# SP's transfers in program order, bias lines on GpSimd, late stores, and a first pair projected side by side

## The chip, the core and the metric

The kernel runs on one core of one Trainium2 chip. TensorE (PE) multiplies matrices into PSUM, VectorE (DVE) and ScalarE (ACT) work on vectors, GpSimd (POOL) does masks and simple sums, and SyncE (SP) issues the transfers between HBM and SBUF. Every engine has its own queue and takes its instructions in order; they meet at semaphores. The metric is the time of one execution in microseconds, as the device measures it; lower is better.

## The reference

One step of a two-layer encoder over 256 prompt frames and 32 sample frames, 288 columns in all, each of 1024 features, in float32:

```
layer 0: x += [chunked attention (8 heads, relative bias) | stick-breaking attention (8 heads)](rmsnorm(x)) @ w_out_ab
layer 1: x += forgetting attention (16 heads, softmax(q k / 8 + cumulative log-forget bias))(rmsnorm(x)) @ w_out_c
each   : x += cross-attention to 256 memory rows (4 heads);   x += (silu(h w_gate) * (h w_up)) w_down
y = rmsnorm(x)
```

The sample frames attend to caches as well. Beside `y` the kernel must return the keys and values of every attention (`kv0`, `kv1`), the log forget values (`lf`) and the memory keys and values (`mkT`, `mv`). The bias of the chunked heads is a table of 257 values a head, indexed by the clipped distance between query and key.

## The kernel before

**Tiles and units.** Activations lie with features on partitions: `x` is 8 tiles of 128 x 288. A weight unit is 128 x 1024 floats (512 KB): the 8 blocks that give 128 output features. Each product is made in three matmuls from a high and a low half (`mm3`, line 145): `unit` (line 132) loads a unit into one of 4 `st` buffers, ScalarE casts it to `hi` (5 buffers), VectorE subtracts to get `lo` (4 buffers). A unit is 24 matmuls; `project` (line 151) does them into one of 4 PSUM banks called `pj`. The normalised input is not scaled by its row's root mean square before the projection: `Next.block` gives x times gain as `hh` and `hl`, and the scale `rstd` (called `cur.r`) is applied when a bank is evicted (`evac_q`, `evac_kv`, `gate`). What is evicted before `rstd` is known waits in a list (`cur.then`).

**Order of work.** The program is one traced sequence. After every unit `project` calls `tick` (line 176), which advances every active generator by one step: norms (`scale`, line 272: `columns`, that is the matmuls `nrm`, then a step later `rows`, that is `nr`), attention heads (`attend_prompt`, line 359: transpose v, scores, softmax; next step transposes `tp`; next step the product `po`), the gate of layer 1 (line 821), memory preparation. A planner then fixes each engine's own order by an estimate of when each instruction is ready and in which order it was traced; it may let an instruction that is ready pass one that is not, on SP too. So in the kernel before, loads may pass stores that wait for their data.

**Start.** `first_part` loads the first unit in three parts between the x tiles (lines 79 to 86). The first three units (q, k and v of pair 0) are projected one after another. 32 small matmuls ahead (line 120) run while the first data arrives. `rel_lines` (line 735) makes the bias table of the chunked heads in DRAM: a line of 384 values a head, written 128 times at a row step of 385, so that rows of 384 read back show it shifted by one each; `rel_prompt` loads two pieces for a head.

**Layers.** `mix_ab` and `mix_c` run `pairs` (line 807): for each of 8 pairs of heads three units, then the pair's attention becomes active, every second pair the sample's too; `memory.steps` puts units of the memory projection between them. `mix_c` first does the gate's unit; the gate's step behind the unit of k0 ends in the two `lf` stores (lines 848, 849), and two steps later it stores cumulative sums in DRAM (`cumd`, `cumsd`), which `attend` of `mix_c` reads back. Then `out_project`, `cross` and `ffn`. In `cross`, `sample` loads four cache tiles into 4 `ca` buffers.

**Names in the profile.** `pj` projections, `op` and `dn` output projections, `mv` memory values, `vt`, `sc`, `tp`, `po` a pair's attention, `gt`, `gc`, `gs`, `gn` the gate, `st` weight loads, `skew` and `bi` the bias.

Of the kernel before, what the change touches and what calls it, by code (L numbers as in the profile page):

```python
# [15 lines left out]
P = 128  # L16
# [6 lines left out]
FB = 22  # L23


@with_exitstack
def encoder_step(ctx: ExitStack, tc: tile.TileContext, a):
# [15 lines left out]
    cnt = [0]  # L43

# [29 lines left out]
    first = wp.tile([P, 1024], F32, tag="st", bufs=4, name="first")  # L74

    def first_part(c0, c1):
        DMA.dma_start(first[:, c0:c1], a["w_ab"][0][:, c0:c1])

    first_part(0, 256)
# [12 lines left out]
    make_identity(nc, identb)  # L92

# [23 lines left out]
    for h in range(4):  # L117
        G.memset(odd[32 * h:32 * h + 32, h % 2:h % 2 + 1], 1.0)

# [12 lines left out]
    def unit(src, st=None, pieces=1):  # L132

        if st is None:
            st = wp.tile([P, 1024], F32, tag="st", bufs=4, name=name("st"))
            DMA.dma_start(st, src)
        hi = wp.tile([P, 1024], F32R, tag="hi", bufs=5, name=name("hi"))
        lo = wp.tile([P, 1024], F32R, tag="lo", bufs=4, name=name("lo"))
        for c in range(pieces):
            b = slice(c * 1024 // pieces, (c + 1) * 1024 // pieces)  # L140
            S.copy(hi[:, b], st[:, b])  # L141
            V.tensor_tensor(lo[:, b], st[:, b], hi[:, b].bitcast(F32), ALU.subtract)  # L142
        return hi, lo
# [7 lines left out]
    def project(src, h, n=NT, w=None, begun=None):  # L151
        if begun:
            w, p = begun
        else:
            w, p = w or unit(src), acc("pj")
        with tc.issue_after(warmed.ins):
            for k in range(BEGIN if begun else 0, KT):
                mm3(p[:, :n], w, k, h, k, k == 0, k == KT - 1)
        tick()
        return p  # L160
# [24 lines left out]
    def finish():  # L185
        while active:
            tick()
# [65 lines left out]
    class Next:  # L253
# [86 lines left out]
    def softmax(s, cols, bias, out):  # L340
# [3 lines left out]
        for i, (c0, c1) in enumerate(cols):  # L344
# [4 lines left out]
            else:  # L349
                V.tensor_tensor_reduce(out=out[:, c0:c1], in0=s[:, c0:c1], in1=bias[:, c0:c1], scale=-1.0, scalar=3e38,  # L350
# [8 lines left out]
    def attend_prompt(q, k, v, vns, j, bias, oh, ol):  # L359

        vn = vns[j] = v_natural(v)
        e = []
        for hd in range(2):
# [5 lines left out]
            softmax(s, QT, bias[hd], e[hd])  # L369
# [134 lines left out]
    def cache(src):  # L504
        t = wk.tile([P, 512], F32, tag="ca", bufs=4, name=name("ca"))
        DMA.dma_start(t, src)
        return t
# [11 lines left out]
    class Memory:  # L519
# [5 lines left out]
        def prepare(self):  # L525

            for c in range(2):
                st = wp.tile([P, 1024], F32, tag="st", bufs=4, name=name("mem"))
                DMA.dma_start(st, a["memT"][:, 1024 * c:1024 * c + 1024])
# [14 lines left out]
        def step(self):  # L544
            i, l = self.i, self.l
            self.i += 1
            if i < 8:
# [5 lines left out]
                DMA.dma_start(a["mkT"][l, i], t[:, 0:NP])  # L553
                self.k.append(split(t[:, 0:NP], tok("kh", F32R)[:, 0:NP], tok("kl", F32R)[:, 0:NP]))
            else:
# [13 lines left out]
                if half == 1:  # L569
                    for t in range(2):  # L570
                        v = tok("mv")
                        V.tensor_scalar(v[:, 0:NP], self.p[:, 256 * t:256 * t + 256], memcol[:, t:t + 1], None, op0=ALU.mult)
                        DMA.dma_start(a["mv"][l, t, :, hd * 256:hd * 256 + 256], v[:, 0:NP])
# [151 lines left out]
    def evac_kv(cur, p, dst):  # L725
        t = tok("kv")

        def go():
            V.tensor_tensor(t, p[:, :NT], cur.r, ALU.mult)
            DMA.dma_start(dst, t)  # L730
# [4 lines left out]
    def rel_lines():  # L735


        ln = cst.tile([8, 384], F32, name="line")
        DMA.dma_start(ln[:, 128:384], a["rel"][:, 0:256])
        V.tensor_copy(ln[:, 0:128], ln[:, 128:129].to_broadcast([8, 128]))  # L740
        d = dr.tile([8, 384], F32, name="lined")
        DMA.dma_start(d, ln)
        sk = dr.tile([8, 128 * 385], F32, name="skew")
        for h in range(8):
            DMA.dma_start(bass.AP(tensor=sk.tensor, offset=sk.offset + h * 128 * 385, ap=[[385, P], [1, 384]]),
                          bass.AP(tensor=d.tensor, offset=d.offset + 384 * h, ap=[[0, P], [1, 384]]))
        return sk

    def rel_rows(sk, h, c, rows, n):

        return bass.AP(tensor=sk.tensor, offset=sk.offset + h * 128 * 385 + c, ap=[[384, rows], [1, n]])

    def rel_prompt(sk, h):
        t = wk.tile([P, 384], F32, tag="bi", bufs=5, name=name("bi"))
        DMA.dma_start(t[:, 0:128], rel_rows(sk, h, 256, P, 128))
        DMA.dma_start(t[:, 128:384], rel_rows(sk, h, 128, P, 256))
        G.memset(t[0:64, 64:128], NEG)
        G.memset(t[0:64, 320:384], NEG)
        return t

    def rel_sample(sk, g):
        t = wk.tile([P, 384], F32, tag="bi", bufs=5, name=name("bs"))
        for h in range(4):
            DMA.dma_start(t[32 * h:32 * h + 32, 0:160], rel_rows(sk, 4 * g + h, 128, NS, 160))
        return t

    def mix_ab(cur, nxt, memory, w0):
# [3 lines left out]

        def proj(j):
            b = 12 * (j // 4) + j % 4
            kv = 8 * (j // 4) + j % 4
            qs[j] = evac_q(cur, project(w[b], cur.h, w=w0 if j == 0 else None))
            if j == 0:
                proj.line = rel_lines()
            ks[j] = evac_kv(cur, project(w[b + 4], cur.h), a["kv0"][kv])
            vs[j] = evac_kv(cur, project(w[b + 8], cur.h), a["kv0"][kv + 4])
# [277 lines left out]
```

## Time and profile before

| what | us |
|---|---|
| runs | 971.6 median of 3 (970.48 to 972.98) |
| the profiled execution: its own time | 974.15 |
| its span, first to last instruction | 972.3 |
| TensorE busy | 955.3 |
| VectorE, ScalarE, GpSimd busy | 588.6, 484.8, 195.1 |
| mean granted clock of TensorE | 0.995 |

Times in the rows are microseconds from the span's start. A row of the list in order of time is: start, duration, engine, line, operation, output<-inputs, shape, count; in brackets the idle time before it and who ended it. A row of stretches has: from:to, length, then busy time and count of PE, weight load (PEld), DVE, ACT and POOL, the clock granted to TensorE, the busy share of the DMA engines and GB/s. A matmul is shown longer than its pace, because matmuls overlap; the pace is the distance between starts. SPq is SP's queue issuing a transfer, not the transfer.

### The profile page before, as it was taken

To read this page: it belongs to the slowest core of one execution; us is meant where nothing else is said; L and a number is where in the kernel's file an instruction comes from. 1 tells how busy PE (TensorE), PEld (TensorE's weight loads), DVE (VectorE), ACT (ScalarE), POOL (GpSimd) and SP (SyncE) were. 2 spreads that over 40 slices of the span, in tenths; PEclk is the share of its full clock that TensorE was granted. 3 is DMA by queue.
4 is the path that set the end of the run, shared out by engine and by line. 5 is a ranking of instruction groups with operands and counts; after the bars stand their busy time and mean duration, and the time that the engine had idled before them with its cause. 6 is when DMAs were issued, how large, how long until landed. Compare 5 with 4: busy or idle time off the path is not lost.

```text
span 972.3 us, 19122 instructions
## 1 busy us (share of the span) xinstructions
PE 955.3 (98%) x7495; PEld 923.2 (95%) x7495; DVE 588.6 (61%) x1133; ACT 484.8 (50%) x856; POOL 195.1 (20%) x291
## 2 busy tenths in 40 slices
PE   8999999999999999999999999999999999999997
PEld 7889999998999999999998999999989999999996
DVE  6587555676666555754565666657757655555452
ACT  5456768545554444444444545446546544444331
POOL 3021001310213222411004333213002222222010
PEclk9999999999999999999999999999999999999999
DMA  7775455544254444554555555555434444444431
GB/s 232 247 241 189 137 180 181 183 162 147 103 174 154 173 162 164 191 192 160 173 202 161 179 190 191 169 164 179 150 117 159 159 159 173 163 164 173 165 117 49
DMA packets 59721, 163.59 MB, mean 168 GB/s; under 512 B 8192, under 2 KB 20528, under 8 KB 59632
## 3 DMA queue, kind: packets, MB, share of 16 engines
q1 hardware_dynamic: 59632, 162.38, 49.0%
q8 instruction: 59, 0.97, 0.4%
q14 instruction: 30, 0.25, 0.1%
HBM read 152.20 MB, written 11.72 MB: 169 GB/s over the span
## 4 chain that ended last, share of the span: by engine, by line
PE 91%; DMA 3%; DVE 3%; issue 1%; ACT 1%; SPq 1%; POOL 0%; DVEq 0%; POOLq 0%; ACTq 0%
PE pj L68 51%; PE dn L68 14%; PE op L68 11%; PE mv L68 5%; PE po L68 1%; PE xo L68 1%; PE xs L68 1%; DMA st<-w_ab 1%; PE zb L68 1%; PE sc L68 1%; DVE lo L142 1%; DMA skew<-lined 1%; DMA x<-xT 1%; PE xss L68 1%; PE xt L614 0%
## 5 line engine op out<-in xcount | busy, mean ns | idle before, releaser
L141 ACT CAST hi<-st 128x1024 fp32r<-128x1024 f32 x260 | 272.2, 1049 | 335.7 <-issue 147.3
L68 PE MATMUL pj<-hh,hi 128*128 128x288 f32 (+1 forms) x1352 | 406.3, 301 | 0.0
L68 PE MATMUL pj<-hl,hi 128*128 128x288 f32 (+1 forms) x1352 | 399.9, 296 | 1.7 <-DVE hl L250 1.7
L68 PE MATMUL pj<-hh,lo 128*128 128x288 f32 (+1 forms) x1352 | 400.2, 296 | 0.0
L142 DVE TENSOR_TENSOR lo<-st,hi 128x1024 fp32r<-128x1024 f32 x260 | 322.7, 1242 | 127.4 <-PE dn L68 41.2
L68 PEld LDWEIGHTS pj<-hh,hi 128*128 128x128 f32 x1352 | 257.0, 190 | 5.8 <-issue 4.2
L68 PEld LDWEIGHTS pj<-hl,hi 128*128 128x128 f32 x1352 | 257.1, 190 | 3.3 <-DVE hl L250 3.2
L68 PEld LDWEIGHTS pj<-hh,lo 128*128 128x128 f32 x1352 | 256.9, 190 | 0.0
L68 PE MATMUL dn<-fh,hi 128*128 128x288 f32 x400 | 108.5, 294 | 0.0
L68 PE MATMUL dn<-fh,lo 128*128 128x288 f32 x352 | 103.3, 294 | 0.0
L68 PE MATMUL dn<-fl,hi 128*128 128x288 f32 x304 | 89.5, 294 | 0.0
L68 PE MATMUL op<-ol,hi 128*128 128x288 f32 x256 | 75.8, 297 | 0.0
L68 PE MATMUL op<-oh,hi 128*128 128x288 f32 x256 | 75.5, 297 | 0.0
L68 PE MATMUL op<-oh,lo 128*128 128x288 f32 x256 | 75.2, 294 | 0.0
L68 PEld LDWEIGHTS dn<-fh,hi 128*128 128x128 f32 x400 | 72.3, 188 | 0.0
L68 PEld LDWEIGHTS dn<-fh,lo 128*128 128x128 f32 x352 | 66.2, 188 | 0.0
L213 POOL TENSOR_TENSOR ssq<-ssq,sq 128x288 f32<-128x288 f32 (+1 forms) x37 | 37.7, 1018 | 119.8 <-ACT sq L202 76.8
L68 PEld LDWEIGHTS dn<-fl,hi 128*128 128x128 f32 x304 | 57.1, 188 | 0.0
L695 POOL TENSOR_TENSOR fl<-us,fh 128x288 fp32r<-128x288 f32 x38 | 32.9, 865 | 119.3 <-ACT fh L694 119.3
L690 DVE TENSOR_TENSOR us<-pj,rstd 128x288 f32<-128x288 f32 x44 | 20.1, 457 | 59.9 <-PE pj L68 59.9
L691 POOL TENSOR_TENSOR gs<-gs,sg 128x288 f32<-128x288 f32 x44 | 38.9, 884 | 75.8 <-ACT sg L689 75.8
L68 PEld LDWEIGHTS op<-ol,hi 128*128 128x128 f32 x256 | 48.2, 188 | 0.6 <-issue 0.4
(257 smaller groups left out, 1204.9 us busy)
## 6 DMA issues: line engine op xcount, KB each, us to landing
st<-w_gate SPq DMA_DIRECT2D x44, 512.0 KB, 3.3
st<-w_up SPq DMA_DIRECT2D x44, 512.0 KB, 3.2
st<-w_down SPq DMA_DIRECT2D x44, 512.0 KB, 3.2
st<-w_c SPq DMA_DIRECT2D x25, 512.0 KB, 3.3
st<-w_ab SPq DMA_DIRECT2D x23, 512.0 KB, 4.4
st<-w_xk SPq DMA_DIRECT2D x16, 512.0 KB, 3.4
st<-w_xv SPq DMA_DIRECT2D x16, 512.0 KB, 3.5
st<-w_xq SPq DMA_DIRECT2D x16, 512.0 KB, 3.5
```

Source lines behind the costliest of these rows:

```text
L68: T.matmul(out, lhsT, rhs, start=start, stop=stop, skip_group_check=True)
L141: S.copy(hi[:, b], st[:, b])
L142: V.tensor_tensor(lo[:, b], st[:, b], hi[:, b].bitcast(F32), ALU.subtract)
L213: eng.tensor_tensor(s[:, :self.n], self.acc[i][:, :self.n], q[:, :self.n], ALU.add)
L690: V.tensor_tensor(us, pu[:, :NT], cur.r, ALU.mult)
L691: G.tensor_tensor(gs, gs, sg, ALU.mult)
L695: G.tensor_tensor(lo, us, hi.bitcast(F32), ALU.subtract)
```

## The change

- Every transfer on SP goes through `move`, which keeps these transfers in the order in which they were traced.
- Stores of keys, values and memory rows go through `store`, which traces them 4 ticks later (`LATE`); `finish` runs until they are out. The gate's stores and `y` use `move` at once.
- All three first units (q, k, v of pair 0) are loaded in three parts each between the x tiles, split as they come, and projected side by side: for each of the 8 blocks 9 matmuls, 3 a unit. One of the three banks is from the `at` set. The scale's `rows` step comes a tick later than before relative to them, behind two further units.
- The bias table is made by GpSimd's transfers at the start, with 64 rows a head instead of 128, in two copies instead of eight; a head's tile is loaded in two halves of 64 partitions, 256 columns wide, when its attention step runs, into the general pool, and the softmax reads it at two column offsets.
- The attention of pair 0 starts two ticks later in `mix_ab` and one in `mix_c` (`later`). Memory preparation becomes active ahead of the third pair, not behind the second.
- `y` is stored in three transfers, not six.

```diff
+LATE = 4
...
+    def move(dst, src):
+        tc.keep_in_program_order(DMA.dma_start(dst, src))
...
+    first = [wp.tile([P, 1024], F32, tag="st", bufs=4, name=f"first{i}") for i in range(3)]
+    def first_part(i, c0, c1):
+        move(first[i][:, c0:c1], a["w_ab"][4 * i][:, c0:c1])
+    PARTS = ((0, 256), (256, 512), (512, 1024))
+    first_part(0, *PARTS[0])
     for i in range(4):
-        DMA.dma_start(xh[i], a["xT"][:, 2 * i * NT:2 * (i + 1) * NT])
+        move(xh[i], a["xT"][:, 2 * i * NT:2 * (i + 1) * NT])
         if i == 0:
-            DMA.dma_start(gain, a["gains"])
-            first_part(256, 512)
-        if i == 1:
-            first_part(512, 1024)
+            move(gain, a["gains"])
+        if i < 3:
+            for u in range(3):
+                if i or u:
+                    first_part(u, *PARTS[i])
...
+    SKEW = 64 * 385
...
+    G.dma_start(line[:, 128:384], a["rel"][:, 0:256])
...
+    G.tensor_copy(line[:, 0:128], line[:, 128:129].to_broadcast([8, 128]))
+    G.dma_start(lined, line)
+    for h in range(0, 8, 4):
+        G.dma_start(bass.AP(tensor=skew.tensor, offset=skew.offset + h * SKEW, ap=[[SKEW, 4], [385, 64], [1, 384]]),
+                    bass.AP(tensor=lined.tensor, offset=lined.offset + 384 * h, ap=[[384, 4], [0, 64], [1, 384]]))
...
     def tick():
...
+        for f in stores.pop(0):
+            f()
+        stores.append([])
+    stores = [[] for _ in range(LATE)]
+    def store(dst, t):
+        stores[-1].append(lambda: move(dst, t))
...
     def finish():
-        while active:
+        while active or any(stores):
             tick()
...
         def scale(self):
-            if self.gi != 1:
+            if self.gi > 1:
                 yield 1
             y = self.norm.columns()
             yield 1
+            if self.gi == 0:
+                yield 1
             p = self.norm.rows(y)
...
-            DMA.dma_start(dst, t)
+            store(dst, t)
...
+    def rel_prompt(h):
+        t = tok("bi")
+        for p in (0, 64):
+            move(t[p:p + 64, 0:256], rel_rows(h, 128 - p, 64, 256))
+        G.memset(t[0:64, 192:256], NEG)
         return t
...
+        def side_by_side():
+            p = [att("pj"), acc("pj"), acc("pj")]
+            with tc.issue_after(warmed.ins):
+                for k in range(KT):
+                    for u in range(3):
+                        mm3(p[u][:, :NT], w0[u], k, cur.h, k, k == 0, k == KT - 1)
+            tick()
+            return p
...
+        def attend(j):
+            return later(attention(j), 2) if j == 0 else attention(j)
...
+            if j == 2 and memory.l == 0:
+                active.append(memory.prepare())
             proj(j)
-            if j == 1 and memory.l == 0:
-                active.append(memory.prepare())
...
-        DMA.dma_start(a["lf"][0:256].rearrange("(t p) h -> p t h", p=P), lf[:, 0:32].rearrange("p (t h) -> p t h", h=H))
-        DMA.dma_start(a["lf"][256:288], lf[0:NS, 32:48])
+        move(a["lf"][0:256].rearrange("(t p) h -> p t h", p=P), lf[:, 0:32].rearrange("p (t h) -> p t h", h=H))
+        move(a["lf"][256:288], lf[0:NS, 32:48])
...
-            return attend_prompt(qs[j], ks[j], vs[j], vns, j, bias, o[0][j], o[1][j])
+            return later(attend_prompt(qs[j], ks[j], vs[j], vns, j, bias, o[0][j], o[1][j]), j == 0)
...
     for m in range(KT):
         cur.block(m, start=True)
-        if m == 1:
-            w0 = unit(None, first, 4)
+        if m in (1, 3, 5):
+            for st, w in zip(first, w0):
+                split_weights(st, w, *PARTS[m // 2])
...
-            DMA.dma_start(a["y"][P * t:min(P * t + P, NT), b], out[r, b])
+        move(a["y"][P * t:min(P * t + P, NT)], out[r])
```

More of the change, by code (lines that the diff above doesn't have):

```diff
@@ L149, in mm3, with project @@
         mm(out, w[1][:, b], h[0][k], False, stop)
[L151 to L158, printed above, removed]
+    def project(src, h, n=NT, begun=None):
+        w, p = begun or (unit(src), acc("pj"))
+        for k in range(BEGIN if begun else 0, KT):
+            mm3(p[:, :n], w, k, h, k, k == 0, k == KT - 1)
         tick()
@@ L338, in v_natural, with softmax @@
         return vn
-    def softmax(s, cols, bias, out):
+    def softmax(s, cols, bias, out, at=None):
         n, rows = len(cols), out.shape[0]
@@ L505, in cache @@
         t = wk.tile([P, 512], F32, tag="ca", bufs=4, name=name("ca"))
[L506 removed]
+        move(t, src)
         return t
@@ L818, in pairs, with later @@
                 memory.steps(steps[j])
+    def later(g, n):
+        for _ in range(n):
+            yield 1
+        yield from g
     def gate(cur, p, res, lf, bf):
```

101 lines of the change are left out of this document (43 added, 58 removed).

## The prediction

> **What bounds the kernel now.** I read first the page, then busy time and granted clock in stretches of 20 us.
>
> ```profile
> span 972.3 us, 19122 instructions
> ...
> PE 955.3 (98%) x7495; PEld 923.2 (95%) x7495; DVE 588.6 (61%) x1133; ACT 484.8 (50%) x856; POOL 195.1 (20%) x291
> ```
>
> ```profile
> 0.00:20.00 20.00, 16.74 (x92) 14.95 (x92) 13.99 (x23) 12.20 (x22) 8.47 (x29) 1.00 0.70 233
> 20.00:40.00 20.00, 17.96 (x125) 16.54 (x127) 8.84 (x32) 5.63 (x15) 1.17 (x8) 0.91 0.79 220
> ...
> 300.00:400.00 100.00, 100.00 (x756) 100.00 (x755) 57.21 (x83) 44.63 (x63) 28.20 (x32) 1.00 0.48 165
> ...
> 500.00:600.00 100.00, 97.03 (x812) 89.43 (x811) 60.38 (x161) 50.46 (x113) 30.89 (x70) 0.98 0.53 179
> ```
>
> TensorE is the bound. From 300 to 400 us it is never idle: 756 matmuls in 100 us, 0.132 us each, so a unit of 24 takes 3.2. Only where TensorE waits, or runs at a lower clock, can this change gain or lose. Such places are the first 40 us (92 and 125 matmuls where 151 would fit in 20 us) and the start of layer 1, just after 500. I then looked at both with stretches of 3.4 us or so, and with the instructions in order of time.
>
> ```profile
> 6.67:10.08 3.41, 3.13 (x11) 2.25 (x10) 2.84 (x5) 2.53 (x6) 2.49 (x5) 1.00 1.02 362
> 10.08:13.49 3.41, 2.33 (x10) 1.98 (x9) 3.41 (x9) 3.19 (x7) 0.83 (x1) 1.00 0.35 137
> 13.49:16.90 3.41, 3.41 (x16) 3.41 (x16) 3.03 (x6) 1.72 (x3) 0.00 (x0) 1.00 0.84 311
> 16.90:20.30 3.40, 3.40 (x29) 3.40 (x29) 2.77 (x4) 1.50 (x3) 0.00 (x0) 1.00 0.85 254
> ...
> 30.50:34.00 3.50, 1.48 (x12) 1.27 (x10) 3.01 (x12) 2.41 (x11) 0.29 (x2) 1.00 0.64 197
> 34.00:37.40 3.40, 3.38 (x15) 2.93 (x16) 1.36 (x6) 2.04 (x5) 0.00 (x0) 0.52 0.43 148
> ...
> 524.00:527.00 3.00, 2.85 (x15) 2.52 (x16) 2.33 (x6) 1.89 (x5) 0.00 (x0) 0.77 0.21 62
> 527.00:530.00 3.00, 3.00 (x16) 2.84 (x15) 0.00 (x0) 0.00 (x0) 0.53 (x2) 0.66 0.71 218
> ```
>
> Up to 16.90 TensorE does about half the matmuls per stretch that it does after, even when fully busy (16 against 29): the pace is about 0.23 us until then, though the clock column already says 1.00. The full pace follows the first stretch that is busy throughout. After a stretch with 42% of work (30.50 to 34.00) the granted clock is 0.52 for one stretch.
>
> ```profile
> 5.13 0.61 PE L68 MATMUL pj<-hh,hi 128*128 128x288 f32 x1
> ...
> 18.82 1.40 PE L68 MATMUL nrm<-mean,ssq 128*128 128x2 f32 x12
> 20.08 0.38 PE L68 MATMUL pj<-hh,hi 128*128 128x288 f32 x1
> ...
> 23.33 0.75 PE L68 MATMUL nr<-ident,y 128*128 128x128 f32 x6
> 23.91 0.38 PE L68 MATMUL pj<-hh,hi 128*128 128x288 f32 x1
> ...
> 33.92 0.30 PE L374 MATMUL tp<-ident,e 128*128 128x128 f32 x1 [2.02 <-DVE e L355]
> ```
>
> The first three units (72 matmuls) take from 5.13 to 23.33, less 1.26 for `nrm`: they would end at 22.07. Then there is a hole of 2.02 us.
>
> **The start: three units side by side.** The same matmuls, reordered so that each pair of x blocks feeds 18 of them instead of 6. The queue now carries 3 x 512 + 4 x 288 + 36 = 2724 KB before the last x. The row of 0 to 20 gives 233 GB/s on average and the stretch from 6.67 a peak of 362, so the last x lands between 10 and 14 us (9.9 with the mean rate up to 6.67 and the peak behind it, 13.7 with 2.0 us of start and the mean throughout); scaling and splitting it adds some 1.4. With 9 matmuls per block of 128 features, 2.1 us at the slow pace, TensorE is busy almost throughout from about 6. If the stretch from 6.67 then counts as busy, about 18 matmuls are done at 10.08 and 54 follow at 0.132: end at 17.2. If the next one does, 33 and 39: 18.6. If only the one that counted before, 48 and 24: 20.1. I take 17.8, between the first two, since the work then in hand leaves no such idle as the 10.08 row shows: **-4.3** (bounds -2.0 and -4.9).
>
> The Trainium skill ("TensorE: Matmul & The Clock Gate", Part 1: The HAM clock gate (the "warmup" mystery)) has a free-running window of about 3.4 us, full rate after one busy window, half rate after an idle one. The stretches agree on the length and on the rise; on the fall they don't, since 42% of work did not keep the clock. By the page's rule the stall priced next would cost no clock, and the sum would be 0.7 lower.
>
> **Behind the three units.** The `nrm` sums need the squares, which VectorE finished in this row:
>
> ```profile
> 18.17 0.45 DVE L213 TENSOR_TENSOR ssq<-ssq,sq 128x288 f32<-128x288 f32 x1
> ...
> 24.92 0.81 DVE L729 TENSOR_TENSOR kv<-pj,rstd 128x288 f32<-128x288 f32 x2
> ```
>
> VectorE and ScalarE have the same splits to do, so they will hardly finish earlier than 18.6: **+0.8** (0 if another unit goes first; 2 if GpSimd's new transfers delay its squares). The row scales move behind two further units, and then q1 and k1 hold the other two of the four `pj` banks, so v1 waits for the first eviction of k0. Before, from `nr` at 23.33 to the first eviction's end at about 25.3 (half of the 0.81) took 2.0, 0.6 of it TensorE's own (to 23.91): **+1.4** (0 if the scales' matmuls get ahead of k1), and for the clock 0.4 x 1.7 = **+0.7** (bounds 0 and 1.7: the stretch would have 59% of work). The 2.02 hole came from an exponential queued behind a late weight split; with `later(..., 2)` and weights queued ahead it goes, with its slow stretch (half of 3.4): **-3.7** (bounds -3.7 and 0). Start together: **-5.1**.
>
> **The bias lines.** 8 copies of 192 KB on SP become two on GpSimd, half the bytes. They fall into the time of the x loads; since they are needed only by the first softmax (about 31 us) I count nothing unless late (a rival below). Memory's preparation, appended ahead of the third pair, has its first step in the same tick as before, and bias tiles from another pool change no order: 0. The y stores become three; the six issues at the end are 3.07 us:
>
> ```profile
> 966.70 3.07 SPq L976 DMA_DIRECT2D y<-yo  x6
> ...
> 508.87 0.40 SPq L848 DMA_DIRECT2D lf<-lf  x1
> ```
>
> Three fewer at 0.5 could end up to 1.5 earlier, but each waits for both halves: **-0.5** (bounds -1.5 and +0.5).
>
> **SP in program order.** This is the edit that can hurt. A transfer that waits now holds all that are traced after it. Late stores: a store waits for its unit's eviction and stands four ticks later, so four units (12.7 us) remain between it and the load behind it. A load needs 3.3 to land and 2.3 for the splits:
>
> ```profile
> st<-w_c SPq DMA_DIRECT2D x25, 512.0 KB, 3.3
> ...
> SPq L136 <- DVE lo L142: 583.8, 218, 10.1
> ```
>
> SP stood 583.8 us waiting for buffers, so it has the room: 0. With one unit of cover instead of four, each store would cost 2.4. In the cross-attention the second cache pair waits for `xso`; behind it now stand the `w_xv` loads:
>
> ```profile
> 230.19 0.81 SPq L506 DMA_DIRECT2D ca<-cmv  x2
> ...
> 236.32 0.28 PE L68 MATMUL mv<-hi,hh 128*128 128x256 f32 x1
> ```
>
> Issued at 231.1, landed at 234.4, split at 235.9: just in time for 236.32, so 0 (bound +1.5 per layer).
>
> **The gate of layer 1** is not covered. Its `lf` stores use `move`, not `store`. They are traced in the tick of k0, so the load of v0 stands behind them on SP, then m0, then `cumd` and `cumsd`, m1, m2.
>
> ```profile
> 467.36 9.84 SPq L136 DMA_DIRECT2D st<-w_c  x4
> ...
> 488.03 0.29 PE L68 MATMUL pj<-hh,hi 128*128 128x288 f32 x1
> ...
> 498.54 0.82 PE L68 MATMUL nr<-ident,y 128*128 128x128 f32 x6
> ...
> 508.89 0.82 PE L68 MATMUL gc<-tri,lf 128*16 128x256 f32 x4 [1.12 <-DVE lf L847]
> ...
> 510.77 0.36 PE L68 MATMUL pj<-hh,hi 128*128 128x256 f32 x1
> ...
> 524.00 0.30 PE L374 MATMUL tp<-ident,e 128*128 128x128 f32 x1 [1.70 <-DVE e L355]
> ```
>
> ```profile
> 495.28 1.23 DVE L142 TENSOR_TENSOR lo<-st,hi 128x1024 fp32r<-128x1024 f32 x1 [0.21 <-issue]
> ...
> 506.84 1.16 DVE L142 TENSOR_TENSOR lo<-st,hi 128x1024 fp32r<-128x1024 f32 x1
> ...
> 508.63 0.21 DVE L847 SCALAR_TENSOR_TENSOR lf<-gate_z,gate_l 128x48 f32<-128x48 f32 x1
> ```
>
> ```profile
> 503.60 1.04 ACT L141 CAST hi<-st 128x1024 fp32r<-128x1024 f32 x1
> ```
>
> Before, four `w_c` loads, v0's among them, were issued from 467 on, more than 20 us before v0's matmuls. Now: TensorE begins at 488.03 with the gate unit, q0 and k0, 72 matmuls, 9.5 us; with `nrm`, `nr` and the transposes, 1.7, it has nothing left at 499.2. The chain from `nr` to the end of `lf` was 498.54 to 508.84, 10.3; without the splits that stood in it (1.04 and 1.16, of loads now held) 8.1; and `nr` comes about 1.2 earlier without the split at 495.28: `lf` at 505.4. Two issues 0.8, the load's own 0.3, landing 3.3, cast 1.05: TensorE goes on at 510.8. That is 11.6 idle, of which the gate's sums (508.89 to 510.77) fill 1.9: 9.7. Then the clock: one to two stretches at half rate, 1.7 to 3.4, say 2.5. Saved is what this stage lost before: 1.12, 1.70, 0.15 in the next transposes, and 1.7 of slow clock (0.23 and 0.34 of 3 us), together 4.7; `later(..., j == 0)` gives the softmax the unit that it lacked. **+7.5** (bounds +5.5 if the chain has no gap at all, +11 if `lf` is no earlier).
>
> **Sum.** -5.1 - 0.5 + 7.5 = +1.9. The profiled execution took 974.15 us (span 972.3), so it would be 976.05; it lies 2.55 above the median of 971.6, for which I forecast **973.5 us**. Differences under 0.3% (2.9 us) can't be told from none here.
>
> **Rivals.**
> (a) The hole at the gate does not open: v0's load goes ahead of `lf`, because the order does not bind it, or the gate ends in time. For it: 20 us of lead before. Against it: the text of the change. Then the stage only gains 3.6 (4.7 less the 1.12): -5.1 - 0.5 - 3.6 = -9.2, **962.4**.
> (b) Slower: a second hole. If TensorE has `gc` behind v0 and m0, as traced, then `cumd` and so m1's load wait for m0. v0 from 510.8 at the slow pace to 516.3, m0 behind it, the sums 1.9, copy and three issues 1.5, landing and cast 4.4: 5.9 idle, the 1.9 no longer hidden, 0.9 of clock: +8.7, **982**. It decides at the place of `gc`; before, it came behind memory matmuls, but it then had no idle TensorE to go to.
> (c) Late bias lines. SP stands at the first bias load, with four of these, six cache and sample loads and then q2's weights behind it, 0.45 each. Before, the eight copies took from 13.74 to 23.07:
>
> ```profile
> 13.74 5.05 SPq L745 DMA_DIRECT2D skew<-lined  x8
> ...
> 16.27 6.79 DMA skew<-lined
> ```
>
> If the two new ones end at 25, q2's load issues at 29.5 and is split at 35, about 3 after TensorE wants it; with the x loads slowed, three units end at 20.1 (+2.3): 1.9 + 2.3 + 3.0 = +7.2, **979**. The Trainium skill ("DMA: Bandwidth & Descriptors", Why a DMA increments its semaphore by 16 and not by 1) lets the slowest dimension set how many of 16 engines a copy uses; here that is 4 where it was 128, which speaks for (c); no run here shows it yet.
> (d) The start yields its bounds (full clock from 10.08, squares and bank hidden) and the hole its lower end: -4.9 - 3.7 - 0.5 + 5.5 = -3.6, **968.0**.
>
> **Chances.** Forecast 0.42, (a) 0.20, (b) 0.11, (c) 0.14, (d) 0.13. The forecast's own range is 969 to 978. Low end 963 (most of (a) inside by half), high end 980 ((c) inside, (b) out). Faster: (a), most of (d) = 0.31. Same: 0.31 of the forecast, 0.04 of (c) and (d) = 0.35. Slower: the rest, 0.34.
>
> **What would show it.** The three units' end near 18; no 2 us wait at the first `tp`; a wait of 1 to 2 us ahead of v1. In layer 1, SP's `lf` stores ahead of a `w_c` load, and TensorE idle about 10 us behind the gate's transposes with a clock near 0.5 after. Without that idle I am wrong by (a).

## The result and the profile after

| | before | after |
|---|---|---|
| median of the runs compared | 971.04 us (970.35 to 972.98) | 1039.72 us (1037.32 to 1043.18) |
| ratio, 95% interval | 1 | 1.0707 (1.0672 to 1.0741) |

The change costs 68.7 us. The forecast was 973.5, with a range up to 980: wrong by 66 us. The first two lines are from the page of the changed kernel's profile.

```profile
span 1038.4 us, 19074 instructions
...
PE 982.3 (95%) x7495; PEld 939.1 (90%) x7495; DVE 597.2 (58%) x1135; ACT 483.7 (47%) x859; POOL 195.5 (19%) x288
```

TensorE does the same 7495 matmuls. It is 27.0 us longer busy (982.3 against 955.3), and its idle time grew from 17.0 to 56.1 us. Where this lies is seen when both kernels are cut at the same places of the program. The rows begin at 40 us, where TensorE has begun 144 weight matmuls in both, and are the rest of layer 0's mixing, then its cross-attention, then (its feed-forward left out, 211.1 and 210.9 us) layer 1's mixing, its cross-attention, and the feed-forward with the end. First the kernel before, then the changed one. The columns are stretch, length, busy time and count of TensorE, of its weight loads, of VectorE, ScalarE and GpSimd, granted clock, DMA share, GB/s.

```profile
40.00:199.10 159.10, 157.82 (x1337) 148.58 (x1334) 103.13 (x212) 107.05 (x197) 27.39 (x34) 1.00 0.58 192
199.10:276.90 77.80, 77.76 (x613) 73.72 (x611) 53.83 (x114) 40.27 (x86) 8.27 (x9) 1.00 0.41 139
...
488.00:672.30 184.30, 181.08 (x1505) 170.18 (x1504) 115.71 (x288) 94.61 (x205) 51.61 (x104) 0.99 0.54 183
672.30:750.20 77.90, 77.85 (x612) 73.78 (x612) 53.83 (x114) 40.34 (x86) 8.31 (x9) 1.00 0.40 139
750.20:972.30 222.10, 214.97 (x1632) 214.40 (x1630) 116.32 (x174) 89.78 (x121) 42.08 (x50) 0.99 0.42 148
```

```profile
40.00:215.60 175.60, 166.56 (x1343) 152.50 (x1344) 106.47 (x216) 108.55 (x201) 26.94 (x30) 0.98 0.48 164
215.60:297.80 82.20, 78.75 (x612) 73.87 (x611) 55.25 (x115) 39.83 (x86) 6.93 (x8) 1.00 0.39 138
...
508.70:734.40 225.70, 201.04 (x1503) 184.04 (x1503) 118.17 (x288) 95.41 (x206) 51.37 (x104) 0.90 0.47 157
734.40:816.30 81.90, 78.99 (x612) 73.92 (x612) 55.28 (x114) 39.94 (x86) 7.45 (x9) 1.00 0.38 132
816.30:1038.40 222.10, 214.97 (x1633) 214.57 (x1631) 116.59 (x174) 89.73 (x121) 42.17 (x50) 0.99 0.43 148
```

The start and layer 0's mixing lost 16.5 us, each cross-attention 4 (82.2 - 77.8 and 81.9 - 77.9), layer 1's mixing 41.4. The feed-forwards, which store nothing and read no caches, lost nothing. In layer 1's mixing half of the loss is idle time (24.7 against 3.2 us) and half is pace: the same number of matmuls is busy 20.0 us longer, at a granted clock of 0.90.

SP's own waits (whom it waited for, total us, times, longest) changed as follows; the first row answers the 583.8 us of before. The row on `kv` was `SPq L730 <- DVE kv L729: 35.8, 24, 3.6`.

```profile
SPq L48 <- DVE lo L158: 419.5, 161, 7.6
SPq L48 <- DVE kv L762: 87.8, 20, 8.5
SPq L48 <- DVE mv L605: 57.8, 14, 13.9
...
SPq L48 <- DVE lf L883: 30.6, 1, 30.6
```

SP now stands more for results (`kv`, `mv`, `lf`) and less for free weight buffers (`lo`), and what is traced behind stands with it. The place of the gate shows both holes that the prediction had named, the forecast's and rival (b)'s. These are SP's transfers there, in order of time, and then TensorE's waits:

```profile
525.70 0.91 SPq L48 DMA_DIRECT2D lf<-lf  x2
526.70 0.37 SPq L48 DMA_DIRECT2D st<-w_c  x1
...
538.73 0.33 SPq L48 DMA_DIRECT2D cumd<-gr  x1
...
539.61 0.85 SPq L48 DMA_DIRECT2D st<-w_xk  x2
```

```profile
525.81 1.44 PE L73 MATMUL gc<-tri,lf 128*16 128x256 f32 x4 [5.64 <-DVE lf L883]
...
531.18 0.61 PE L73 MATMUL pj<-hh,hi 128*128 128x288 f32 x1 [1.79 <-ACT hi L157]
...
544.27 0.55 PE L73 MATMUL pj<-hh,hi 128*128 128x256 f32 x1 [2.33 <-ACT hi L157]
```

### The profile page after: what moved, and what is told of

Its sections match the earlier page's. It is cut to its first block, busy times and chain, and to the rows that moved or that the text cites. A ratio compares the mean times of both kernels' runs of the same rounds, so it can differ in the third digit from the quotient of the medians.

```text
span 1038.4 us, 19074 instructions
## 1 busy us (share of the span) xinstructions
PE 982.3 (95%) x7495; PEld 939.1 (90%) x7495; DVE 597.2 (58%) x1135; ACT 483.7 (47%) x859; POOL 195.5 (19%) x288
## 4 chain that ended last, share of the span: by engine, by line
PE 78%; DMA 7%; ACT 7%; DVE 5%; issue 2%; SPq 1%; DVEq 0%; ACTq 0%
PE pj L73 46%; PE dn L73 13%; PE op L73 8%; PE mv L73 3%; ACT hi L157 2%; DVE lo L158 2%; DMA st<-w_ab 2%; DMA st<-w_xv 1%; PE po L73 1%; DMA st<-w_xk 1%; DMA st<-w_oab 1%; SPq L48 1%; ACT e L384 1%; PE sc L73 1%; DMA st<-w_xo 1%
## 5 line engine op out<-in xcount | busy, mean ns | idle before, releaser
L73 PE MATMUL pj<-hh,lo 128*128 128x288 f32 (+1 forms) x1352 | 405.7, 300 | 3.0 <-DVE lo L158 3.0
L73 PE MATMUL pj<-hl,hi 128*128 128x288 f32 (+1 forms) x1352 | 404.3, 299 | 0.0
L157 ACT CAST hi<-st 128x1024 fp32r<-128x1024 f32 x258 | 269.0, 1049 | 244.6 <-issue 80.6
L73 PEld LDWEIGHTS pj<-hh,hi 128*128 128x128 f32 x1352 | 262.1, 194 | 11.0 <-ACT hi L157 5.7
L73 PEld LDWEIGHTS pj<-hh,lo 128*128 128x128 f32 x1352 | 261.3, 193 | 6.8 <-DVE lo L158 5.4
L73 PEld LDWEIGHTS pj<-hl,hi 128*128 128x128 f32 x1352 | 262.2, 194 | 0.0
L348 POOL TENSOR_TENSOR kl<-mk,kh 128x256 fp32r<-128x256 f32 x16 | 15.0, 935 | 205.1 <-ACT kh L347 195.0
```

The source lines that it names most:

```text
L73: T.matmul(out, lhsT, rhs, start=start, stop=stop, skip_group_check=True)
L157: S.copy(hi, st[:, c0:c1])
L348: eng.tensor_tensor(lo, t, hi.bitcast(F32), ALU.subtract)
```

## The experiments

**The order undone, and the order alone.** `a_free` is the changed kernel with one line different; `g_order_alone` is the kernel before with `move` and `store` and nothing else of the change.

```diff
# a_free, against the changed kernel
-        tc.keep_in_program_order(DMA.dma_start(dst, src))
+        DMA.dma_start(dst, src)
# g_order_alone, against the kernel before: all transfers but the bias table's
-            DMA.dma_start(st, src)
+            move(st, src)
...
-            DMA.dma_start(dst, t)
+            store(dst, t)
```

> The changed kernel with one thing undone: its transfers on SP may pass each other again, as before; the start, the late stores, the bias on GpSimd and the rest stay. Theory 1 (program order on SP is the loss: loads stand behind transfers that wait for a computation): 955 to 975 us, that is before less up to 5 us of the start. Theory 2 (the loss is in the rest of the change: side by side start, later attention of pair 0, bias tiles from the general pool): 1020 to 1040.

> The kernel before with program order on SP and stores four ticks late as the only edits (the bias table's own transfers stay free). Theory 1: 1025 to 1050 us, nearly all of the loss. Theory 2: 965 to 985.

Measured: `a_free` 984.97 us, ratio 1.0118 (1.0103 to 1.0133); `g_order_alone` 1039.63 us, ratio 1.067 (1.0647 to 1.0693). Program order (with the late stores, which `a_free` has too) is the loss, and without it 57 of the 69 us are gone by the ratios. But `a_free` is 10 us above what theory 1 gave it. I compared the start of every 24th weight matmul in both traces: from the twentieth unit on, its distance to before stays between 8 and 9.5 us (less at the gate), so what it lacks lies in the start, a second question, below. The same distance shows where `g_order_alone` loses: from the gate's unit to the end it grows by 43 us, in the changed kernel by 45. Only the starts differ, 10 us at the eleventh unit with the old one against 7.

**Which transfers.** I held the late stores, or the gate's stores, for the ones that hold the loads, and freed them.

```diff
# c_stores_free
-        stores[-1].append(lambda: move(dst, t))
+        stores[-1].append(lambda: DMA.dma_start(dst, t))
# d_gate_free
-        move(a["lf"][0:256].rearrange("(t p) h -> p t h", p=P), ...)
+        DMA.dma_start(a["lf"][0:256].rearrange("(t p) h -> p t h", p=P), ...)
# ... and so for lf's second part, cumd and cumsd
```

> The changed kernel with only the stores of keys, values and memory rows free to be passed; loads, the gate's stores and y stay in order. Theory 1 with the late stores as the main cause: of the 68 us, the gate's holes (13 to 24) and cross (8) stay and the rest goes, so 995 to 1010. Theory 1 with the gate's and the read-back transfers as the main cause: 1025 to 1040. Theory 2: 1035 to 1040.

> The changed kernel with only the gate's four stores (lf twice, cumd, cumsd) free. Theory 1 with the late stores as the main cause: the two holes of the gate go, 13 to 24 us, so 1015 to 1027. Theory 1 with the gate as the cause of all that layer 1's mixing lost (41.6 us): about 998. Theory 2: 1035 to 1040.

Measured: 1042.6 us, ratio 1.0695 (1.0656 to 1.0734), and 1040.94 us, ratio 1.0682 (1.0645 to 1.0718): nothing gained, an outcome that my expectation gave to theory 2 as well, and that `a_free` rules out. SP's transfers in `d_gate_free` around the gate show why:

```profile
500.20 0.33 SPq L48 DMA_DIRECT2D st<-w_c  x1
531.19 0.40 SPq L884 DMA_DIRECT2D lf<-lf  x1
...
532.20 0.37 SPq L48 DMA_DIRECT2D st<-w_c  x1
```

The two `lf` stores are free here (they have lines of their own), yet the load of v0 still stands behind them. Freeing a store lets the store move; the load, kept in order, stays behind whatever was traced ahead of it. That is read from these rows; the next two runs test it. The loads had to be freed:

```diff
# h_weights_free: in unit(), and the same for memT
-        move(st, src)
+        DMA.dma_start(st, src)
# n_gate_loads: only the first twelve units of layer 1's mixing
+        if 127 < len(units) <= 139:
+            DMA.dma_start(st, src)
+        else:
+            move(st, src)
```

> The changed kernel with the loads of weights and of the memory free to be traced past; every other transfer (stores, bias, caches, gate) stays in program order. Freeing the stores alone gave nothing, since a load kept in order still holds its place behind whatever is traced ahead of it. Theory 1 (it is the place of the weight loads that costs, whatever it is they stand behind): 980 to 990 us, as with all transfers free. Rival 3 (the kept stores, bias tiles and caches themselves come late): over 1005.

> The changed kernel with only the first twelve weight loads of layer 1's mixing free; everything else stays in program order, the gate's four stores too. If the gate's holes come from the place of these loads behind lf, cumd and cumsd: the holes go (TensorE was stopped for 13 to 24 us there), so 1015 to 1025, and what is lost later in this stage stays. If TensorE stops there for another reason (the gate's own chain): 1034 to 1040.

Measured: `h_weights_free` 980.82 us, ratio 1.0082 (1.0066 to 1.0099): all of the order's loss goes when only the weight loads are free, and SP waits for weight buffers again (SP's waits in this kernel):

```profile
SPq L163 <- DVE lo L158: 597.8, 222, 10.1
SPq L48 <- DVE kv L762: 41.7, 21, 10.0
```

`n_gate_loads` 1022.05 us, ratio 1.0493 (1.047 to 1.0515), in its first range. Against the changed kernel's ratio that is 0.0214 of 972, about 21 us, for twelve loads: the gate's two holes with the slow matmuls behind them. The loads now go first, then `lf`:

```profile
518.16 7.05 SPq L166 DMA_DIRECT2D st<-w_c  x3
...
537.21 0.91 SPq L49 DMA_DIRECT2D lf<-lf  x2
```

The place itself says the same. These are the stretches from the gate's unit to the start of the fifteenth unit behind it, with the same 489 matmuls, of the kernel before, the changed kernel and `n_gate_loads`:

```profile
488.03:551.80 63.77, 60.80 (x489) 56.38 (x487) 38.01 (x99) 31.15 (x60) 15.58 (x33) 0.97 0.55 183
508.52:594.14 85.62, 71.19 (x489) 63.84 (x487) 38.17 (x97) 30.30 (x59) 15.67 (x33) 0.84 0.40 129
516.35:577.12 60.77, 59.39 (x489) 54.95 (x487) 37.15 (x97) 29.12 (x59) 14.21 (x33) 1.00 0.50 154
```

The changed kernel loses 21.9 us here, and with these loads free nothing is lost.

**Why four units of cover did not do.** Two runs change how far a load stands behind what it may have to wait for, with everything in program order.

```diff
# e_late10
-LATE = 4
+LATE = 10
# p_ahead2: UNITS is a table of the 258 units in the order of their use
+AHEAD = 2
...
-        st = wp.tile([P, 1024], F32, tag="st", bufs=4, name=name("st"))
-        move(st, src)
+        while todo and len(waiting) <= AHEAD:
+            n, i = todo.pop(0)
+            t = wp.tile([P, 1024], F32, tag="st", bufs=4, name=name("st"))
+            at = bass.AP(tensor=WT[n].tensor, offset=i * P * 1024, ap=[[1024, P], [1, 1024]])
+            move(t, at)
+            waiting.append((t, at))
+        st, at = waiting.pop(0)
```

> The changed kernel with stores traced ten ticks late in place of four; all transfers in program order. Theory 1 with the stores as what the loads stand behind: mixing of layer 0 loses under 5 us in place of 16, the steady part of layer 1's mixing loses nothing, the gate's holes (13 to 24) and cross (8) stay: 990 to 1010. With bias, cache and gate transfers as what they stand behind: 1025 to 1040.

> The changed kernel, all transfers in program order, with each weight load traced two units earlier (a table of the 258 units in their order says which is next; four buffers as before). Theory 1: the time from a load's issue to its first matmul, 15 us median in mixing against 25 before, gains most of the 6.4 us of two units and the loss shrinks by more than half: 975 to 1000. If program order costs through something else than the lead of the loads: 1025 to 1040.

Measured: `e_late10` 1035.07 us, ratio 1.0646 (1.0614 to 1.0679), a miss for theory 1 as I had put it; `p_ahead2` 987.78 us, ratio 1.0155 (1.0138 to 1.0173), as it expects. I worked out the lead of the weights from the traces: from the issue of a load to the first of its 24 matmuls, loads and groups of 24 paired from the end of the program backward, medians in us:

| kernel | layer 0 mixing | cross | feed-forward | layer 1 mixing | ratio |
|---|---|---|---|---|---|
| before | 25.0 | 30.0 | 20.5 | 27.1 | 1 |
| after | 15.0 | 16.0 | 20.4 | 16.6 | 1.0707 |
| weights free | 25.7 | 30.0 | 20.4 | 27.1 | 1.0082 |
| two units ahead | 20.0 | 22.4 | not worked out | 20.9 | 1.0155 |
| stores ten ticks late | 24.1 | 16.1 | not worked out | 20.8 | 1.0646 |

The lead fell by 10 us in mixing and by 14 in cross, and not where nothing was lost. With stores ten ticks late, layer 0's mixing has its lead back, and there the loss stops (from the tenth to the fiftieth unit the distance to before grows by 4 us, in the changed kernel by 9). But the stores were not the only transfers that wait. SP's waits in `e_late10`:

```profile
SPq L48 <- DVE lo L158: 497.5, 196, 8.0
...
SPq L48 <- DVE st L385: 35.7, 3, 16.3
...
SPq L48 <- PE po L73: 24.5, 3, 10.2
```

The 87.8 us for `kv` are gone (0.4 remain), and in their place SP stands until a buffer of the softmax (`st`) or of a head's output (`po`) is free; where it stands longest in this stage, a read-back `ck` or the weight load behind it is the next to issue. `lf`, `cumd` and the cross-attention's caches stand as before. So no single store was the cause: any transfer in the line that waits for attention takes the place of the last. Loads traced two units earlier get round most of them at once; half of what is left then is the gate, whose holes are longer than two units (the distance to before grows by 7 us there).

**What a shorter lead costs.** The prediction asked only whether the weights arrive in time. That they do not is about a third of the 39.1 us of added idle time: TensorE waited directly for splits for 7.1 us in projections (4.1 for `hi`, 3.0 for `lo`), 5.6 in the memory's values and 0.7 in the output projections, 13.4 in all, where the list of before has no such wait. What else it lost is seen in two places of the changed kernel. First, an attention without a projection to cover it:

```profile
566.16 0.61 PE L73 MATMUL sc<-kv,q 64*128 64x256 f32 x4
...
566.94 0.26 PE L73 MATMUL ss<-kv,q 64*32 64x32 f32 x8
568.88 0.30 PE L407 MATMUL tp<-ident,e 128*128 128x128 f32 x1 [1.69 <-DVE e L387]
```

The scores (`sc`, and the sample's `ss`) are followed at once by the transposes that need their softmax. Twelve such waits for `e` make 13.1 us, against 5.0 in six before. The stretches around this one (columns as above) show what follows it:

```profile
567.40:570.80 3.40, 1.30 (x6) 0.68 (x6) 2.46 (x14) 2.57 (x11) 0.40 (x1) 1.00 0.14 42
570.80:574.20 3.40, 2.31 (x7) 1.14 (x7) 2.40 (x6) 3.40 (x7) 0.00 (x0) 0.62 0.00 0
574.20:577.60 3.40, 3.40 (x16) 3.40 (x17) 1.95 (x2) 0.88 (x1) 0.00 (x0) 0.50 0.42 154
577.60:581.00 3.40, 3.40 (x25) 3.40 (x24) 1.56 (x2) 1.36 (x2) 1.13 (x1) 0.87 0.18 51
```

After a stretch with 38% of work the clock falls to 0.62 and 0.50: 16 matmuls in a stretch that is busy throughout, where about 26 fit. With the 0.87 that follows, these make 6.9 us at half rate, two stretches. That is how 21 us of idle time in this stage became 41. The Trainium skill ("TensorE: Matmul & The Clock Gate", HAM oscillation — how this bites in real kernels) describes the same for waits on data and puts the limit at idle gaps above about 3.4 us; here gaps of 1.69 and 1.52 us with work between them were enough, so the measurement is stricter than the page.

Second, ScalarE takes its queue in order and stood at a cast whose load was late, with an exponential behind it (and a table load of 1.28 us between the two):

```profile
104.91 0.91 SPq L48 DMA_DIRECT2D ca<-cab  x2
105.92 0.38 SPq L48 DMA_DIRECT2D st<-w_xk  x1
...
111.21 1.05 ACT L157 CAST hi<-st 128x1024 fp32r<-128x1024 f32 x1 [4.37 <-DMA st<-w_xk]
...
113.57 0.87 ACT L490 ACTIVATE sw<-zb 128x384 f32<-128x384 f32 x2
...
114.11 1.25 PE L73 MATMUL po<-sw,vn 128*64 128x256 f32 x8 [1.14 <-ACT sw L490]
```

How the loss divides between these two was not tried: that the planner put attention without cover because it reckoned with later weights is argued from the order, not shown.

**The start.** `a_free` stood 8.7 us behind before at its ninth unit. TensorE waited 9.2 us for the squares of the first norm, which ScalarE had behind casts. I held those casts back, then mended more of the same kind, and put the old start back.

```diff
# l_squares, against a_free: casts of the fourth to eighth loaded unit
+            with tc.issue_after(squares[3].ins):
+                split_weights(st, w)
# m_start_tuned, against a_free
+        with tc.issue_after(squares[3].ins) if 1 <= n <= 8 else nullcontext():
             S.copy(hi, st[:, c0:c1])
+        with tc.issue_after(ys[2].ins) if 2 <= n <= 8 else nullcontext():
             V.tensor_tensor(lo, st[:, c0:c1], hi.bitcast(F32), ALU.subtract)
...
-            p = [att("pj"), acc("pj"), acc("pj")]
+            p = [att("pj"), att("pj"), acc("pj")]
# s_old_start, against a_free: first unit alone in parts, three units one after another
-            p = side_by_side() if j == 0 else (project(w[b + 4 * i], cur.h) for i in range(3))
+            p = (project(w[b + 4 * i], cur.h, begun=(w0, acc("pj")) if j == i == 0 else None, ...) for i in range(3))
# m3, against m_start_tuned
-        with tc.issue_after(ys[2].ins) if 2 <= n <= 8 else nullcontext():
+        with tc.issue_after(evicted[1].ins) if len(evicted) > 1 and 4 <= n <= 8 else tc.issue_after(ys[2].ins) if 2 <= n <= 8 else nullcontext():
...
-                return attend_prompt(*args, lambda: [rel_prompt(2 * j + i) for i in range(2)], ...)
+                return attend_prompt(*args, [rel_prompt(2 * j + i) for i in range(2)], ...)
...
+        with tc.issue_after(loads[2].ins) if len(caches) <= 4 else nullcontext():
             move(t, src)
```

> The changed kernel with all transfers free (985 us) and, on ScalarE, the casts of the fourth to eighth loaded unit held behind the four squares of the first norm. With all transfers free the first norm's product waited 9.2 us for these squares, since casts stood ahead of them. If this is why that kernel was 12 us slower than before: 970 to 977, and 964 to 970 if the start then gains the 4 us that the changed kernel shows at its fifth unit. If the start is slow for another reason: 982 to 986.

> The changed kernel with all transfers free and three edits at the start: ScalarE's four squares of the first norm ahead of the casts of all loaded units, VectorE's subtractions of the second to eighth loaded unit behind the end of the norm's chain (the last y), and two of the side by side banks from the general set in place of one. Before this the kernels with free transfers lost 8 us at nr, 1.4 at a bank, and ran the next 14 matmuls at half rate. If the start's loss is these three and nothing else: 966 to 972, the first version faster than before. If the start loses by something else: 976 to 981.

> The changed kernel with all transfers free and the start of the kernel before: one unit loaded in parts, the first pair's three units one after another, the norm's rows and the first attention at their old steps. Bias lines on GpSimd, bias tiles from the general pool, late stores, memory preparation and the three stores of y stay as changed. If the 12 us that the kernel with free transfers lost are all of the side by side start: 969 to 974. If the bias tiles, the pool or the other small edits cost: 976 to 985.

> The version with the tuned start (978 us) and three edits: bias tiles traced when the attention is made, not when it runs; the first four cache loads behind the third weight load; VectorE's subtractions of the fourth to eighth unit behind the first evictions. In the run before this one TensorE waited 3.1 us at vt for an eviction that stood behind subtractions, and the bias tiles were issued 18 us later than in the kernel before. If these are what is left of the loss: 970 to 974. If not: 976 to 980.

Measured: `l_squares` 980.6 us, ratio 1.008 (1.0065 to 1.0095), a miss: its wait moved on to 8.1 us at `nr`, behind VectorE's subtractions. `m_start_tuned` 978.07 us, ratio 1.0057 (1.0044 to 1.0071), in its second range, so the three edits do not cover the start's loss: the wait moved again, to 2.1 us for the fourth unit's cast and 3.1 for an eviction. `s_old_start` 990.11 us, ratio 1.0185 (1.0171 to 1.0198), outside both ranges: putting the old start back made it worse, so these kernels with free transfers don't measure the start. In it the first bias tiles were issued at 45.3 us, where before had them at 20.4 (they are traced in the attention step now), and TensorE lost 4.2 us at `tp`. `m3` 980.19 us, ratio 1.0078 (1.0062 to 1.0095), a miss too: tiles traced early again, still 4.3 us lost at an eviction. So I put the start alone on the kernel before:

```diff
# u_start_alone, against the kernel before: the start of the changed kernel, nothing else
+        def side_by_side():
+            p = [att("pj"), acc("pj"), acc("pj")]
...
+            active.append(later(attend(j), 2) if j == 0 and memory.l == 0 else attend(j))
# v_start_chain, against u_start_alone
+            p = [att("pj"), att("pj"), acc("pj")]
...
+        with tc.issue_after(ys[2].ins) if 2 <= len(units) <= 8 else nullcontext():
             V.tensor_tensor(lo, st[:, c0:c1], hi.bitcast(F32), ALU.subtract)
# w_half_table, against v_start_chain: 64 rows a head, and loads of units 4 to 7 first
+                for u in (1, 5, 9, 2):
+                    early.append(wp.tile([P, 1024], F32, tag="st", bufs=4, name=name("st")))
+                    proj.last = DMA.dma_start(early[-1], w[u])
+                with tc.issue_after(proj.last.ins):
+                    proj.line = rel_lines()
...
-        sk = dr.tile([8, 128 * 385], F32, name="skew")
+        sk = dr.tile([8, 64 * 385], F32, name="skew")
```

> The kernel before with the side by side start alone (three units loaded in parts, projected side by side, norm rows a step later, first attention two steps later); bias table, stores and order of transfers as before. If the step of the forecast holds by itself (three units end 4.3 us earlier, the 2.02 us wait and its slow stretch go, banks and clock cost 2 to 3): 966 to 969. If the start is bound by the arrival of data, so that what the three units gain the fourth waits for: 971 to 975. If the side by side start is the cause of what the kernels with free transfers lost: 977 to 984.

> As the run before, with two edits: VectorE's subtractions of the second to eighth loaded unit stand behind the end of the norm's chain, and two of the three banks come from the general set. If these two stalls (up to 2.3 us at nr, 1.4 at the bank, and the slow matmuls behind them) are what the start alone loses: 2 to 5 us below the run before. If not: the same.

> The run with the start alone and its chain mended, with the changed kernel's bias table of 64 rows a head (half the bytes, still on SP), and the seventh unit's load issued ahead of the table's copies and of the first caches. If the wait of 6.2 us for the seventh unit's weights comes from the place of its load behind 1.5 MB of bias copies and the caches: it goes, and the time is 967 to 971. If all loads of the start are bound by their bytes, the wait moves to the next unit's weights: 972 to 976.

Measured: 974.35 us, ratio 1.0023 (1.0013 to 1.0032); 973.74 us, ratio 1.0013 (1.0004 to 1.0023); 972.79 us, ratio 0.9997 (0.9988 to 1.0006). All three lie where the expectations had put a start that gains nothing. In `u_start_alone` the 2.02 us wait of before is gone, and this one is there:

```profile
30.23 1.82 SPq L767 DMA_DIRECT2D bs<-skew  x4
32.15 0.37 SPq L145 DMA_DIRECT2D st<-w_ab  x1
...
36.28 1.04 ACT L139 CAST hi<-st 128x1024 fp32r<-128x1024 f32 x1 [7.82 <-DMA st<-w_ab]
...
37.38 0.61 PE L68 MATMUL pj<-hh,hi 128*128 128x288 f32 x1 [3.31 <-ACT hi L139]
```

The seventh unit's load is issued at 32.15, behind the bias copies, the bias and sample tiles. Three units done earlier only mean that TensorE comes sooner to weights that come no sooner. `w_half_table` puts that load first and halves the copies: the 3.3 us (6.2 in `v_start_chain`) shrink to 0.7 at a later unit, but 1.6 us open at a `tp`, and its time cannot be told from before. No version was faster than the kernel before.

## Why the prediction was wrong

**SP in program order and late stores: priced 0, the step that failed.** The term was "four units (12.7 us) remain between it and the load behind it. A load needs 3.3 to land and 2.3 for the splits ... so it has the room: 0". The cover was sized about rightly in the median (a lead of 15.0 us for 12.7), though 6 of the 32 loads behind that median had less than 12.7, one 5.7; waits for the weights themselves are 13.4 of the 39.1 us of added idle time. The main mistake was the other side: 5.6 us is what a load needs, not what the kernel used. It had used 25. With two units more of lead, in the same program order, 54 of the 69 us come back. That the rest of the lead let ScalarE cast ahead of the exponentials and gave TensorE a projection between scores and transposes fits the two places above; how much each is worth stays open. The sentence that read SP's 583.8 us of waiting as room read it backwards: SP waiting for `lo` means that loads are issued as early as the buffers allow. That is the good state; the changed kernel has 419.5. Also, the step looked only at the store of four units ago; ten ticks of delay instead of four gave back only 0.6% of the 7.1%, since other transfers in the line wait as well. What this step costs: all of the loss that is neither the gate's (about 21 us) nor cross's (8), some 36 to 40 us.

**The gate: +7.5, right in place, a third of the size (21.9).** `lf` was forecast at 17.4 us from the start of the stage (505.4 - 488.03) and stood at 17.0 (525.70 - 508.70); v0's matmuls were forecast at 22.8 and came at 22.5 (531.18 - 508.70). But rival (b) was not a rival: its hole opened too. The prediction had made a case of its own, at 0.11, of something that the same text had traced to the same cause. 7.5 and 8.7 together are 16.2, still short of 21.9. The idle time was sized about rightly: 14.4 us in the stretch above, 3.2 of it the two waits of the attention at 568 to 572, against 9.7 + 5.9. The term that was too small is the clock: a mean of 0.84 over 85.62 us is 27 us at half rate, where the 2.5 and the 0.9 of the two cases stand for 7.

**Cross: 0, bound +1.5 a layer; measured 4.4 and 4.0.** The place was right. SP's transfers in the changed kernel, then TensorE's wait:

```profile
246.60 1.06 SPq L48 DMA_DIRECT2D ca<-cmv  x2
247.78 0.83 SPq L48 DMA_DIRECT2D st<-w_xv  x2
```

```profile
254.79 0.38 PE L73 MATMUL mv<-hi,hh 128*128 128x256 f32 x1 [1.89 <-ACT hi L157]
```

The failed term is the landing: the first `w_xv` load, issued with two caches and three other weight loads within 2.6 us, landed 5.9 us after its issue, not 3.3. TensorE waited 1.89 us for its cast and 0.88 more for its subtraction, and 1.12 and 0.88 in layer 1. How the rest of the 4.4 and 4.0 divides was not worked out. An estimate that comes out just in time is a cost, not a zero.

**The start: -5.1; alone it measured +1.75 (974.35 against 972.6).** In the changed kernel the seventh unit begins 3.3 us later than before. The three units did end near 18: their last matmul starts at 18.2 us. The bank's stall was 1.44 (forecast 1.4). But `nr` waited 2.26 more, and the 2.02 us at the first `tp` did not go (the changed kernel):

```profile
28.58 1.20 PE L73 MATMUL nr<-ident,y 128*128 128x128 f32 x6 [2.26 <-DVE y L261]
...
31.22 0.58 PE L73 MATMUL pj<-hh,hi 128*128 128x288 f32 x1 [1.44 <-DVE kv L762]
...
39.89 0.33 PE L407 MATMUL tp<-ident,e 128*128 128x128 f32 x1 [2.02 <-DVE e L387]
```

The failed terms are the -3.7 for that hole, and the clock: from 28 to 34 us the granted clock was 0.58, about 5 us at half rate, where the +0.7 stands for 1.4. Where the hole did go, in the start alone, a wait for weights took its place: I had not asked what TensorE meets next when it arrives 4 us earlier.

**Bias lines: 0, rival (c) +7.2.** (c) was half right: SP stood 6.2 us until the first of the two copies had landed and went on at 19.94, and in the stretch from 18 to 22 us the DMA engines were at a share of 0.44 where before had 0.97. But TensorE's list of the first 60 us in the changed kernel has no wait for splits longer than 0.51 us, so (c)'s 3 us did not come. The eight copies of 192 KB landed 6.9 us (median) after their issue, the two of 384 KB 9.4.

**y: -0.5; measured 0.** The last stage takes 222.10 us in both. **Rival (a)** needed loads that the order does not bind; it binds them.

## What to carry to other kernels

Before an order is fixed in a queue of loads, measure the lead that the loads have now, from issue to first use, and ask what uses it; a queue that waits for buffers is not idle room but a sign that it runs as far ahead as it can. If a queue is to keep its order, trace each load earlier by the lead it must have: two units earlier gave back 54 of 69 us, while releasing the transfers in front of the loads gave back nothing. Work done earlier at a start gains only if the data for the work behind it comes earlier too.

## What the hardware showed

Holes of 1.5 to 2 us with some work around them are enough to halve TensorE's pace for one or two stretches of 3.4 us (38% busy, then 0.62, 0.50 and 0.87), and in layer 1's mixing the loss was about twice the added idle time (41.4 us for 21.4). I had expected one to two slow stretches from a hole, not that a series of such holes takes the granted clock of a whole stage of 226 us to 0.90. Cut where the clock changes, into stretches of 3.41 us, the changed kernel's trace shows the border: of its stretches at full rate all that were at most 53% busy were followed by half rate, and none from 57% up; at half rate, one that was at most 93% busy was followed by another slow one, and one that was busy throughout by full rate. In `g_order_alone` the border is less sharp (51% kept the full rate once, 64% once did not). And fewer, larger copies of the bias table were not faster: 768 KB in two took longer to land (9.4 us each) than each of eight of 192 KB (6.9), with half the total. The Trainium skill ("DMA: Bandwidth & Descriptors", Why a DMA increments its semaphore by 16 and not by 1) would have 4 of 16 engines work on a copy whose slowest dimension is 4; the longer landing agrees with it, though another queue issued them, other loads ran at the same time and no run here counts the engines.
